# The end of a down projection on one Trainium2 core: plain products joined to the last group's PSUM sums, and a norm for each token tile

## The chip, the cores and the metric

One NeuronCore of a Trainium2 chip. The metric is the device time of one execution in microseconds (us); three runs of the kernel before took 749.31, 750.06 and 750.24 us, median 750.06 us. TensorE, VectorE, ScalarE and GpSimd appear in the profile as PE, DVE, ACT and POOL, and SP issues DMAs.

## The reference, cut to what matters

One decoder layer over 512 tokens of width 1024. The change is in the last two lines of the layer and in the final norm:

```python
u = rms_norm(h, norm_ffn_g[l])
g, up = jnp.split(u @ w_gate_up[l], 2, axis=-1)     # 1024 -> 2 x 2816
h = h + (jax.nn.silu(g) * up) @ w_down[l]           # 2816 -> 1024
return rms_norm(h, norm_final_g)                    # over the 1024 columns of each token
```

All of it is float32.

## The kernel before

Every float32 operand of a matmul is split in a high and a low part of a reduced type (fp32r), and a product is three matmuls: high by high, high by low, low by high. ScalarE writes the high part (a copy) and VectorE the low part (a subtraction). What precedes the down projection (the mixers, the output projection, 22 gate/up items) is not touched, but for one line of `gu_last`.

The hidden width of 2816 is 22 k-tiles of 128. The first 20 stand in five groups of four, `ds` 0 to 4. A group is multiplied by a seven-product scheme (Strassen's, in Winograd's form) over a 2 x 2 split: tokens in two halves (256 each), k-tiles in two, output columns in two halves of 512. Its seven products have the names of their weights, W11, S1, S2, W12, S3, S4 and W22. Of these S1 to S4 are sums of weight blocks, made by VectorE in `ds_prep` (L770), then split by ScalarE and VectorE (L775). Each product is done for two token tiles of 128 (t = 0, 1, with t + 2 in the other half) by `ds_prod`: two k-tiles by three matmuls with 512 columns. X (two PSUM tiles, `mm`) takes W11, then S2, S3 and W22 on top, and is read after each; Z (two tiles, `s`) takes S1, then S4 on top; W12 has a tile of its own (`acc`).

Groups 0 to 3 add their results to the residual in DRAM. `ds_end` is the last group, the two last k-tiles (20 and 21, `LK` = 2) and the final norm. `end_load` has brought the residual back to eight SBUF tiles `hs[t][j]` of 128 tokens by 512 columns (t = 0 to 3, j = 0, 1), and the norm's gain to `g3[j]`. In `ds_end`:

- `add_` (L975, VectorE) adds a PSUM tile, times the token's factor `r` or `nr` = -r, to an `hs` tile.
- The two last k-tiles (`LAST`, L1019 to L1030) are plain products: for each of the eight (t, j) a PSUM tile of its own, six matmuls (L1026 to L1028) and one `add_`. They stand between S2 and W12.
- The final norm goes by pairs of token tiles, (0, 1) and (2, 3). ScalarE squares each `hs` tile with a running sum. For four of the eight tiles `early` lets GpSimd multiply by the gain (L985). `rstd_pair` makes the reciprocal root of a pair (ScalarE's Ln and Exp, then Newton's step in three small VectorE instructions, L319 to L321). `apply` scales one half by root and gain on VectorE (L1000), the other, already multiplied by the gain, by the root on ScalarE, and issues the stores, 256 KB each, from SP and one of them from ScalarE.

The order is made by a scheduler at build time: `plan` lays the products out on a clock of priorities, and `at(key, product, offset)` sets the priority of what follows; each engine then works its list in that order, and waits at the first instruction that isn't ready.

Of the kernel before, what the change touches and what calls it, by code (L numbers as in the profile page):

```python
# [15 lines left out]
P = 128  # L16
# [55 lines left out]
NG = 5  # L72
DS_AFTER = {4: 0, 8: 1, 12: 2, 16: 3, 21: 4}

H_OFF, L_OFF, S_OFF, U_OFF, E_OFF, O_OFF, D_OFF = 1800, 800, 3800, 0, 3000, 1500, 1500
# [9 lines left out]
def hybrid_layer_kernel(ctx: ExitStack, tc, xT, wall, wgu, wds, wdl, g3v, vecs, wgates, consts, rope, out):  # L85
# [616 lines left out]
    def plan():  # L702

        t = 0
        seq = [(ITEMS[0], "W11")]
        for j, x in enumerate(ITEMS):
            if j == len(ITEMS) - 1:
                seq += [(x, w) for w in ("S1", "S2", "LAST", "W12", "S3", "W22", "S4")]
                continue
# [3 lines left out]
        for x, w in seq:  # L713
            clock["at"][x, w] = t
            t += 1440 if x[0] == "gu" else 8 * 680 * LK if w == "LAST" else 2720
# [42 lines left out]
    def ds_prep(n):  # L758
# [3 lines left out]
        for k in DS_W if n < NG - 1 else DS_W[:3] + (0, 1) + DS_W[3:5] + DS_W[:4:-1]:  # L762
# [3 lines left out]
            if k[0] == "S":  # L766
                a, b = {"S1": ("W21", "W22"), "S2": ("S1", "W11"), "S3": ("W11", "W21"), "S4": ("S2", "W12")}[k]
                at(key, k, -S_OFF)
# [73 lines left out]
    def gu_last(i):  # L842
# [14 lines left out]
        if i >= 4 * NG:  # L857
            V.tensor_tensor(u, u, t, op=ALU.mult)
# [103 lines left out]
    def ds_end():  # L962

        n = NG - 1
# [5 lines left out]
        v_ = lambda: small([P, 2], "v2")  # L970
        ss = {(x, j): v_() for x in (0, 2) for j in two}

        def add_(t, j, ps, c):

            V.scalar_tensor_tensor(hs[t][j], ps, c, hs[t][j], op0=ALU.mult, op1=ALU.add)  # L975

        def square(t, j):
            x = t % 2
            act_(slot(name="sq"), hs[t][j], AF.Square, accum_out=ss[t - x, j][:, x : x + 1])

        def early(t, j):

            at(key, "S4")
            square(t, j)
            nc.gpsimd.tensor_tensor(hs[t][j], hs[t][j], g3[j], op=ALU.mult)  # L985

        def rstd_pair(t0):

            v, q, z = v_(), v_(), ss[t0, 0]
            V.tensor_tensor(z, z, ss[t0, 1], op=ALU.add)  # L990
            act_(q, z, AF.Ln, scale=1.0 / D, bias=epsc)
            V.tensor_scalar(v, z, 1.0 / D, EPS, op0=ALU.mult, op1=ALU.add)
            act_(q, q, AF.Exp, scale=-0.5)
            return newton(q, v, v_)

        def apply(t0, j, q):

            for x in two:
                t, c = t0 + x, q[:, x : x + 1]
                V.scalar_tensor_tensor(hs[t][j], hs[t][j], c, g3[j], op0=ALU.mult, op1=ALU.mult)  # L1000
                act_(hs[t][1 - j], hs[t][1 - j], AF.Copy, scale=c)
                for e in two:
                    (nc.scalar if t == 3 and e != j else nc.sync).dma_start(out[t][:, e * S : e * S + S], hs[t][e])
# [15 lines left out]
        for t in range(4):  # L1019
            for j in range(2):  # L1020
                at(key, "LAST", (2 * t + j) * 1360)
                ps = mmb() if j else accb()
                q, c = slice(t * P, (t + 1) * P), slice(j * S, (j + 1) * S)
                for k in range(LK):
                    (ah, al), (wh, wl) = hid[k], DL[k]
                    T.matmul(ps, ah[:, q], wh[:, c], start=k == 0, stop=False)  # L1026
                    T.matmul(ps, ah[:, q], wl[:, c], start=False, stop=False)
                    T.matmul(ps, al[:, q], wh[:, c], start=False, stop=k == LK - 1)  # L1028
                at(key, "LAST", (2 * t + j) * 1360 + D_OFF)
                add_(t, j, ps, r[t])  # L1030
# [559 lines left out]
```

## Time and profile before

| | |
|---|---|
| three runs, median | 750.06 us (749.31 to 750.24) |
| the profiled execution, its own time | 749.53 us |
| its span, from first to last instruction | 747.8 us |
| PE busy | 734.0 us, 98% of the span, 4230 instructions |
| DVE busy | 624.0 us, 83% |
| ACT busy | 430.6 us, 58% |
| POOL busy | 66.0 us, 9% |
| mean granted clock of TensorE | 0.996 |

The span lies 1.73 us below the profiled execution's own time. The views used below are: the page's busy times; the timeline of one engine, where a row is a start, a duration, and an instruction, and a bracket gives the idle time before it and what ended it; the windows, which sum busy time over a stretch; and the groups by line. Matmuls overlap in the array: a matmul of 512 columns lasts 0.39 us from start to end, but the next one starts 0.23 us after it, so the distance between starts is what counts. The same holds on DVE and ACT, where the next start comes some 0.08 us before the end that is shown.

### The profile page before, as it was taken

How to read it: one execution, taken by the hardware profiler on the slowest of the kernel's cores; microseconds unless marked ns; L12 is line 12 of the kernel's file. 1: busy time of each engine (PE TensorE's matmuls, PEld its weight loads, DVE VectorE, ACT ScalarE, POOL GpSimd, SP SyncE). 2: the span in 40 equal slices, each digit the busy share in tenths (PEclk: the TensorE clock that was granted, in tenths of full speed). 3: DMA queues.
4: the chain of work that ended last, by engine and by line, in shares of the span. 5: the costliest groups of instructions: out<-in, count | busy, mean ns of one | idle time of the engine just before them, and what ended most of it. 6: DMA issues, size and time to landing. Idle time of an engine off the chain costs nothing.

```text
span 747.8 us, 11429 instructions
## 1 busy us (share of the span) xinstructions
PE 734.0 (98%) x4230; PEld 635.9 (85%) x4230; DVE 624.0 (83%) x1065; ACT 430.6 (58%) x739; POOL 66.0 (9%) x82
## 2 busy tenths in 40 slices
PE   9999999999999999999999999999999999999994
PEld 5788888888888888888888998899899899899983
DVE  6897776799986787566778899899999999988896
ACT  7534767578755437523447565665655765665534
POOL 0002010000000000000000000400400210220003
PEclk9999999999999999999999999999999999999998
DMA  9777654222432213524777253983985796496403
GB/s 332 270 227 206 185 178 121 101 106 78 134 135 84 85 57 104 178 96 130 188 183 194 99 163 105 231 255 74 234 251 125 180 283 157 119 251 197 140 1 113
DMA packets 50839, 118.70 MB, mean 159 GB/s; under 512 B 4944, under 2 KB 9688, under 8 KB 50784
## 3 DMA queue, kind: packets, MB, share of 16 engines
q1 hardware_dynamic: 36832, 88.82, 35.0%
q0 software_dynamic: 9440, 26.77, 18.2%
q10 hardware_dynamic: 4512, 2.39, 1.1%
q8 instruction: 33, 0.54, 0.3%
q14 instruction: 22, 0.18, 0.1%
HBM read 101.16 MB, written 16.81 MB: 158 GB/s over the span
## 4 chain that ended last, share of the span: by engine, by line
PE 94%; DVE 2%; ACT 1%; DMA 1%; issue 1%; SPq 0%; DVEq 0%; ACTq 0%
PE mm L201 12%; PE mm L202 12%; PE mm L203 12%; PE mm L783 6%; PE mm L785 6%; PE mm L784 6%; PE s L783 3%; PE s L785 3%; PE s L784 3%; PE mm L894 3%; PE mm L896 2%; PE mm L895 2%; PE mm L471 2%; PE mm L470 2%; PE acc L1309 1%; PE mm L472 1%
## 5 line engine op out<-in xcount | busy, mean ns | idle before, releaser
L148 ACT ACTIVATE wh<-raw 128x1024 fp32r<-128x1024 f32 x58 | 61.3, 1058 | 67.6 <-PE mm L202 65.0
L161 DVE TENSOR_TENSOR wl<-raw,wh 128x1024 fp32r<-128x1024 f32 x58 | 70.4, 1219 | 9.9 <-ACT wh L148 9.2
L783 PE MATMUL mm<-bq,w 128*128 128x256 f32 x264 | 76.1, 288 | 0.4
L785 PE MATMUL mm<-bq,w 128*128 128x256 f32 x264 | 74.7, 283 | 0.0
L784 PE MATMUL mm<-bq,w 128*128 128x256 f32 x264 | 74.6, 283 | 0.0
L148 ACT ACTIVATE w<-s 128x1024 fp32r<-128x1024 f32 x44 | 46.6, 1060 | 35.0 <-DVE s L740 16.2
L731 DVE TENSOR_TENSOR w<-s,w 128x1024 fp32r<-128x1024 f32 x44 | 53.8, 1222 | 9.4 <-ACT w L148 7.6
L201 PE MATMUL mm<-u,wh 128*128 128x512 f32 x136 | 55.0, 405 | 0.3 <-DVE ga L563 0.3
L693 POOL DMA_DIRECT2D s<-in_wgu_dram x22 | 19.5, 888 | 396.4 <-DVE ga L585 133.2
L203 PE MATMUL mm<-u,wh 128*128 128x512 f32 x136 | 53.3, 392 | 0.0
L783 PEld LDWEIGHTS mm<-bq,w 128*128 128x128 f32 x264 | 50.5, 191 | 3.2 <-ACT x L148 1.9
L202 PE MATMUL mm<-u,wl 128*128 128x512 f32 x136 | 53.2, 391 | 0.0
L203 PE MATMUL mm<-ul,wh 128*128 128x512 f32 x136 | 53.0, 390 | 0.0
L202 PE MATMUL mm<-uh,wl 128*128 128x512 f32 x136 | 53.0, 390 | 0.0
L201 PE MATMUL mm<-uh,wh 128*128 128x512 f32 x136 | 52.9, 389 | 0.0
L784 PEld LDWEIGHTS mm<-bq,w 128*128 128x128 f32 x264 | 50.6, 192 | 0.1
L785 PEld LDWEIGHTS mm<-bq,w 128*128 128x128 f32 x264 | 50.6, 192 | 0.0
L148 ACT ACTIVATE w<-raw 128x1024 fp32r<-128x1024 f32 (+2 forms) x45 | 43.4, 974 | 12.1 <-PE s L784 5.9
L783 PE MATMUL s<-bq,w 128*128 128x256 f32 x176 | 50.2, 285 | 0.0
L785 PE MATMUL s<-bq,w 128*128 128x256 f32 x176 | 49.9, 283 | 0.0
L784 PE MATMUL s<-bq,w 128*128 128x256 f32 x176 | 49.8, 283 | 0.0
L148 ACT ACTIVATE w<-sw 128x1024 fp32r<-128x1024 f32 x20 | 21.2, 1062 | 33.8 <-DVE sw L770 33.5
(398 smaller groups left out, 2242.1 us busy)
## 6 DMA issues: line engine op xcount, KB each, us to landing
raw<-in_wall_dram SPq DMA_DIRECT2D x59, 512.0 KB, 3.9
s<-in_wgu_dram SPq DMA_DIRECT2D x22, 512.0 KB, 4.4
s<-in_wgu_dram POOLq DMA_DIRECT2D x22, 512.0 KB, 6.1
raw<-in_wgu_dram SPq DMA_DIRECT2D x22, 512.0 KB, 4.1
raw<-in_wds_dram SPq DMA_DIRECT2D x20, 512.0 KB, 9.5
w<-in_wgu_dram SPq DMA_DIRECT2D x22, 256.0 KB, 7.6
h1d<-s POOLq DMA_DIRECT2D x16, 256.0 KB, 10.0
R<-scr POOLq DMA_DIRECT2D x4, 896.0 KB, 4.8
```

Source lines behind the costliest of these rows:

```text
L148: return A.activation(out_, in_, func, **kw)
L161: V.tensor_tensor(l, src, f(h), op=ALU.subtract)
L201: T.matmul(ps, wh[:, c], rh[j], start=start and j == 0, stop=False)
L202: T.matmul(ps, wl[:, c], rh[j], start=False, stop=False)
L203: T.matmul(ps, wh[:, c], rl[j], start=False, stop=stop and j == n - 1)
L470: T.matmul(ps, uh[k][:, c], h, start=k == 0, stop=False)
L693: nc.gpsimd.dma_start(s13, wgu[i][:, 512:1536].rearrange("p (x c) -> p x c", x=2), accum_op=ALU.add)
L731: V.tensor_tensor(dst[1], src, f(dst[0]), op=ALU.subtract)
L783: T.matmul(ps, wh[:, c], bh, start=first and k == 0, stop=False, skip_group_check=not first)
L784: T.matmul(ps, wl[:, c], bh, start=False, stop=False, skip_group_check=not first)
L785: T.matmul(ps, wh[:, c], bl, start=False, stop=k == 3, skip_group_check=not first)
L894: T.matmul(ps, bh, wh[:, d], start=first and k == 0, stop=False, skip_group_check=not first)
```

## The change

- **Plain products join sums.** In `gu_last` the hidden values of k-tiles 20 and 21 are negated for the upper 256 tokens. `last(ps, t, j)` puts the six matmuls of LAST for one (t, j) on top of a sum that is added to the same `hs` tile with the same sign anyway: (0,0) and (1,0) with W12, (0,1) and (1,1) with W22, (2,0) and (3,0) with S4. Only (2,1) and (3,1) keep a tile of their own. That of (3,1) is cut in two halves of 256 columns; the second is the last product of the kernel.
- **The end is ordered by token tile.** `ds_prod` of W22 and S4 goes tile by tile, 0, 1, 2, 3, each followed by LAST, `add_`, `square`, `rstd` and `apply` of that tile; the last product is for token tile 3.
- **A norm for each token tile.** `rstd` works on one column (128 x 1) and not two. The last square's sum goes in as the input of Ln, the other sums and epsilon as its bias.
- **Nothing on GpSimd.** `times_g` (L1007 in the new file) multiplies by the gain on VectorE.
- **Priorities.** `plan` puts W12 before S3 before LAST, with new lengths; the weight sum of the last S4 comes 10000 ahead of its product and not 3800.

The lines that are taken out stand in the functions above; these are the ones that are put in, with a line of "..." where others are left out:

```diff
-H_OFF, L_OFF, S_OFF, U_OFF, E_OFF, O_OFF, D_OFF = 1800, 800, 3800, 0, 3000, 1500, 1500
+H_OFF, L_OFF, S_OFF, U_OFF, E_OFF, O_OFF, D_OFF, S4_OFF = 1800, 800, 3800, 0, 3000, 1500, 1500, 10000
...
+        LONG = {"W12": 4, "LAST": 1, "W22": 4, "S4": 5}
-                seq += [(x, w) for w in ("S1", "S2", "LAST", "W12", "S3", "W22", "S4")]
+                seq += [(x, w) for w in ("S1", "S2", "W12", "S3", "LAST", "W22", "S4")]
-            t += 1440 if x[0] == "gu" else 8 * 680 * LK if w == "LAST" else 2720
+            t += 1440 if x[0] == "gu" else 1360 * LONG.get(w, 2) if x == ITEMS[-1] else 2720
...
-                at(key, k, -S_OFF)
+                at(key, k, -S_OFF if k != "S4" or n < NG - 1 else -S4_OFF)
...
-            V.tensor_tensor(u, u, t, op=ALU.mult)
+            V.tensor_tensor(u[:, A_], u[:, A_], t[:, A_], op=ALU.mult)
+            V.scalar_tensor_tensor(u[:, B_], u[:, B_], -1.0, t[:, B_], op0=ALU.mult, op1=ALU.mult)
...
-        at(ITEMS[-1], "LAST", -H_OFF)
+        at(ITEMS[-1], "W12", -H_OFF)
...
+        ss = {}
+        U = 1360
+        v_ = lambda: small([P, 1], "v1")
+        def add_(t, j, ps, c, d=slice(0, S)):
+            h = hs[t][j][:, d]
+            V.scalar_tensor_tensor(h, ps[:, d], c, h, op0=ALU.mult, op1=ALU.add)
+        def square(t, j, d=slice(0, S)):
+            s = v_()
+            act_(slot(name="sq")[:, d], hs[t][j][:, d], AF.Square, scale=D**-0.5, accum_out=s)
+            ss.setdefault(t, []).append(s)
+        def rstd(t, w_, o):
+            at(key, w_, o - 600)
+            *s, e = ss[t]
+            z, v, q = v_(), v_(), v_()
+            i = V.tensor_scalar(z, s[0], s[-1] if len(s) > 1 else 0.0, EPS, op0=ALU.add, op1=ALU.add)
+            at(key, w_, o)
+            act_(q, e, AF.Ln, bias=z)
+            V.tensor_tensor(v, e, z, op=ALU.add)
+            return q, v, (i, act_(q, q, AF.Exp, scale=-0.5))
+        def apply(t, q, j):
+            V.scalar_tensor_tensor(hs[t][j], hs[t][j], q, g3[j], op0=ALU.mult, op1=ALU.mult)
+            act_(hs[t][1 - j], hs[t][1 - j], AF.Copy, scale=q)
+            for e in (j, 1 - j):
+                (nc.scalar if t == 3 and e != j else nc.sync).dma_start(out[t][:, e * S : e * S + S], hs[t][e])
+        def times_g(t, j):
+            V.tensor_tensor(hs[t][j], hs[t][j], g3[j], op=ALU.mult)
+        def last(ps, t, j, first=False, d=slice(0, S)):
+            q, c = slice(t * P, (t + 1) * P), slice(j * S + d.start, j * S + d.stop)
+            for k in range(LK):
+                (ah, al), (wh, wl) = hid[k], DL[k]
+                g = dict(skip_group_check=not first)
+                T.matmul(ps[:, d], ah[:, q], wh[:, c], start=first and k == 0, stop=False, **g)
+                T.matmul(ps[:, d], ah[:, q], wl[:, c], start=False, stop=False, **g)
+                T.matmul(ps[:, d], al[:, q], wh[:, c], start=False, stop=k == LK - 1, **g)
...
         for t in two:
+            at(key, "W12", 2 * U * t)
+            y = accb()
+            last(y, t, 0, first=True)
+            ds_prod(y, w["W12"], n, 2, t)
+            at(key, "W12", 2 * U * (t + 1) + D_OFF)
+            add_(t, 0, y, r[t])
+            square(t, 0)
+        for t in two:
+            at(key, "S3", U * t)
+            ds_prod(X[t], w["S3"], n, 5, t)
+            at(key, "S3", U * t + D_OFF)
+            add_(t + 2, 1, X[t], r[t + 2])
+        for t in two:
+            at(key, "W22", U * t - 1000)
             add_(t + 2, 1, Z[t], r[t + 2])
+        at(key, "LAST")
+        y = accb()
+        last(y, 2, 1, first=True)
+        at(key, "W22", 2000)
+        add_(2, 1, y, nr[2])
+        square(2, 1)
         for t in two:
+            at(key, "W22", 2 * U * t)
             ds_prod(X[t], w["W22"], n, 6, t)
+            last(X[t], t, 1)
+            at(key, "W22", 2 * U * t + 1000)
+            times_g(t, 0)
+            at(key, "W22", 2 * U * (t + 1) + 200)
             add_(t, 1, X[t], r[t])
             square(t, 1)
+            q, v, _ = rstd(t, "W22", 2 * U * (t + 1) + 2000)
+            apply(t, newton(q, v, v_), 1)
+        at(key, "S4")
+        ds_prod(Z[0], w["S4"], n, 3, 0)
+        last(Z[0], 2, 0)
+        at(key, "S4", 1000)
+        times_g(2, 1)
+        at(key, "S4", 2 * U + 200)
+        add_(2, 0, Z[0], nr[2])
+        square(2, 0)
+        q, v, _ = rstd(2, "S4", 2 * U + 2000)
+        q2 = newton(q, v, v_)
+        y = accb()
+        lo, hi = slice(0, HS), slice(HS, S)
+        at(key, "S4", 2 * U)
+        last(y, 3, 1, first=True, d=lo)
+        at(key, "S4", 3 * U)
+        add_(3, 1, y, nr[3], lo)
+        square(3, 1, lo)
+        at(key, "S4", 5 * U // 2)
+        ds_prod(Z[1], w["S4"], n, 3, 1)
+        last(Z[1], 3, 0)
+        at(key, "S4", 9 * U // 2 + 200)
+        add_(3, 0, Z[1], nr[3])
+        square(3, 0)
+        at(key, "S4", 9 * U // 2)
+        last(y, 3, 1, first=True, d=hi)
+        at(key, "S4", 5 * U + 200)
+        add_(3, 1, y, nr[3], hi)
+        square(3, 1, hi)
+        q, v, i = rstd(3, "S4", 5 * U + 800)
+        with tc.issue_after(raw_ins(i[0])), tc.issue_after(raw_ins(i[1])):
+            apply(2, q2, 0)
+            times_g(3, 0)
+        apply(3, newton(q, v, v_), 1)
```

What the scheduler makes of it, at the three places on which the prediction rests. Names: `h_7448` to `h_7455` are hs[0][0], hs[0][1], hs[1][0] and so on to hs[3][1]; `mm_..` with h_7449, h_7451, h_7453 or h_7455 is X, `s_..` is Z, `acc_..` a tile for W12 or LAST; `sw` is a sum of weight blocks and `w` a split of one; `v` are the norm's small columns, `g` the gain.

First place, VectorE between the additions of S3 and the split of S4's weights. Before:

```order
L975 SCALAR_TENSOR_TENSOR h_7453<-mm_7608,rc_4001,h_7453 128x512
L770 TENSOR_TENSOR sw_7383<-sw_7355,raw_7097 128x1024
L975 SCALAR_TENSOR_TENSOR h_7455<-mm_7609,rc_4001,h_7455 128x512
L975 SCALAR_TENSOR_TENSOR h_7449<-mm_7608,rc_4001,h_7449 128x512
L775 TENSOR_TENSOR w_7386<-sw_7383,w_7385 128x1024
L975 SCALAR_TENSOR_TENSOR h_7451<-mm_7609,rc_4001,h_7451 128x512
L975 SCALAR_TENSOR_TENSOR h_7452<-s_7610,nrc_4002,h_7452 128x512
```

Now:

```order
L771 TENSOR_TENSOR sw_7383<-sw_7355,raw_7097 128x1024
L981 SCALAR_TENSOR_TENSOR h_7453<-mm_7606,rc_4001,h_7453 128x512
L981 SCALAR_TENSOR_TENSOR h_7455<-mm_7607,rc_4001,h_7455 128x512
L981 SCALAR_TENSOR_TENSOR h_7453<-s_7608,rc_4001,h_7453 128x512
L981 SCALAR_TENSOR_TENSOR h_7455<-s_7609,rc_4001,h_7455 128x512
L1007 TENSOR_TENSOR h_7448<-h_7448,g_7446 128x512
L981 SCALAR_TENSOR_TENSOR h_7453<-acc_7700,nrc_4002,h_7453 128x512
L981 SCALAR_TENSOR_TENSOR h_7449<-mm_7606,rc_4001,h_7449 128x512
L1007 TENSOR_TENSOR h_7450<-h_7450,g_7446 128x512
L993 TENSOR_SCALAR v_7728<-v_7664 128x1
L776 TENSOR_TENSOR w_7386<-sw_7383,w_7385 128x1024
L996 TENSOR_TENSOR v_7729<-v_7725,v_7728 128x1
```

The sum for S4 (sw_7383) stood behind X's first addition of S3 and ahead of the second; it now stands ahead of both. The split of its low part (w_7386) now stands behind the addition into h_7449, which waits for W22 and LAST of token tile 0, and two multiplies by the gain (L1007), which were GpSimd's, are in the line.

Second place, the end of TensorE's list (L894 to L896 are `ds_prod`, in the new file L897 to L899; L1015 to L1017 are `last`). Before, the last rows:

```order
L896 MATMUL s_7610<-w_7385,acl_7332 128x512
L895 MATMUL s_7611<-w_7386,ach_7058 128x512
L896 MATMUL s_7611<-w_7385,acl_7059 128x512
L894 MATMUL s_7611<-w_7385,ach_7331 128x512
L895 MATMUL s_7611<-w_7386,ach_7331 128x512
L896 MATMUL s_7611<-w_7385,acl_7332 128x512
```

Now, the last rows:

```order
L1017 MATMUL s_7609<-w_7361,acl_7512 128x512
L1015 MATMUL s_7609<-w_7365,ach_7602 128x512
L1016 MATMUL s_7609<-w_7366,ach_7602 128x512
L1017 MATMUL s_7609<-w_7365,acl_7603 128x512
L1015 MATMUL acc_7804<-w_7361,ach_7511 128x256
L1016 MATMUL acc_7804<-w_7362,ach_7511 128x256
L1017 MATMUL acc_7804<-w_7361,acl_7512 128x256
L1015 MATMUL acc_7804<-w_7365,ach_7602 128x256
L1016 MATMUL acc_7804<-w_7366,ach_7602 128x256
L1017 MATMUL acc_7804<-w_7365,acl_7603 128x256
```

Before, the last product is S4 of tile 3, and LAST is long done. Now LAST for (3, 0) follows S4 in the same PSUM tile, and the last six rows are the second half of LAST for (3, 1), 256 columns each. The first half stands 54 rows ahead, between S3 and W22. TensorE has 96 rows of 512 columns in this stretch before, and 90 of 512 and 12 of 256 now.

Third place, the end of VectorE's list. Before:

```order
L975 SCALAR_TENSOR_TENSOR h_7454<-s_7611,nrc_4002,h_7454 128x512
L319 TENSOR_TENSOR v_7785<-v_7779 128x2
L320 SCALAR_TENSOR_TENSOR v_7785<-v_7785,v_7778 128x2
L321 SCALAR_TENSOR_TENSOR v_7785<-v_7785,v_7779 128x2
L1000 SCALAR_TENSOR_TENSOR h_7449<-h_7449,v_7785,g_7447 128x512
L1000 SCALAR_TENSOR_TENSOR h_7451<-h_7451,v_7785,g_7447 128x512
L990 TENSOR_TENSOR v_7606<-v_7606,v_7607 128x2
L992 TENSOR_SCALAR v_7815<-v_7606 128x2
L319 TENSOR_TENSOR v_7821<-v_7816 128x2
L320 SCALAR_TENSOR_TENSOR v_7821<-v_7821,v_7815 128x2
L321 SCALAR_TENSOR_TENSOR v_7821<-v_7821,v_7816 128x2
L1000 SCALAR_TENSOR_TENSOR h_7452<-h_7452,v_7821,g_7446 128x512
```

Now:

```order
L319 TENSOR_TENSOR v_7800<-v_7795 128x1
L981 SCALAR_TENSOR_TENSOR h_7455<-acc_7804,nrc_4002,h_7455 128x256
L320 SCALAR_TENSOR_TENSOR v_7800<-v_7800,v_7794 128x1
L321 SCALAR_TENSOR_TENSOR v_7800<-v_7800,v_7795 128x1
L993 TENSOR_SCALAR v_7841<-v_7812,v_7828 128x1
L1001 SCALAR_TENSOR_TENSOR h_7452<-h_7452,v_7800,g_7446 128x512
L996 TENSOR_TENSOR v_7842<-v_7838,v_7841 128x1
L1007 TENSOR_TENSOR h_7454<-h_7454,g_7446 128x512
L319 TENSOR_TENSOR v_7853<-v_7843 128x1
L320 SCALAR_TENSOR_TENSOR v_7853<-v_7853,v_7842 128x1
L321 SCALAR_TENSOR_TENSOR v_7853<-v_7853,v_7843 128x1
L1001 SCALAR_TENSOR_TENSOR h_7455<-h_7455,v_7853,g_7447 128x512
```

Before, behind the last addition (h_7454) stand two Newton steps of three rows and four multiplies by root and gain, of which the last, for h_7454, follows these rows. Now the last addition is the half of h_7455, and behind it stand the rest of tile 2's Newton step and all of tile 3's, one multiply by root and gain for each of the two tiles, and one multiply by the gain alone. On the GpSimd list the four rows of L985 are gone, and nothing is put there.

## Rows read from the trace of the kernel before

**Rows 1.** The page, its first line.

```profile
span 747.8 us, 11429 instructions
```

**Rows 2.** TensorE's timeline, last 23.5 us: start, duration, instruction, idle before it.

```profile
714.49 0.39 PE L1026 MATMUL acc<-w,ach 128*128 128x512 f32 x1
...
731.97 0.39 PE L896 MATMUL mm<-w,ac 128*128 128x512 f32 x1
733.31 0.50 PE L894 MATMUL mm<-w,ac 128*128 128x512 f32 x1 [0.96 <-DVE h L975]
...
737.54 0.40 PE L896 MATMUL s<-w,acl 128*128 128x512 f32 x1
```

**Rows 3.** The timeline of TensorE's weight loads: a wait in product S4.

```profile
735.34 0.19 PEld L895 LDWEIGHTS s<-w,ach 128*128 128x128 f32 x1 [0.34 <-DVE w L775]
```

**Rows 4.** VectorE's timeline where the sum for S4 is made.

```profile
730.34 2.26 DVE L770 TENSOR_TENSOR sw<-sw,raw 128x1024 f32<-128x1024 f32 x1
732.52 1.39 DVE L975 SCALAR_TENSOR_TENSOR h<-mm,rc,h 128x512 f32<-128x512 f32 x2
```

**Rows 5.** Groups by line and form, 714 to 738: the same sum without GpSimd.

```profile
L770 DVE TENSOR_TENSOR sw<-raw,raw 128x1024 f32<-128x1024 f32 x1 | 1.2, 1217 | 0.0
```

**Rows 6.** GpSimd's timeline, three of its four multiplies by the gain.

```profile
728.91 4.82 POOL L985 TENSOR_TENSOR h<-h,g 128x512 f32<-128x512 f32 x3 [56.26 <-ACT sq L148]
```

**Rows 7.** VectorE's timeline behind the last product.

```profile
741.31 0.16 DVE L319 TENSOR_TENSOR v<-v 128x2 f32<-128x2 f32 x1 [0.40 <-ACT v L153]
...
741.90 1.42 DVE L1000 SCALAR_TENSOR_TENSOR h<-h,v,g 128x512 f32<-128x512 f32 x2
```

**Rows 8.** SP's store issues; windows (length, busy times, clock, DMA share, GB/s); landing of stores.

```profile
740.00 4.02 SPq L1003 DMA_DIRECT2D out_dram<-h  x7
740.50:741.00 0.50, 0.00 (x0) 0.00 (x0) 0.38 (x3) 0.47 (x2) 0.00 (x0) 1.00 0.29 106
742.00:743.00 1.00, 0.00 (x0) 0.00 (x0) 1.00 (x2) 1.00 (x2) 0.00 (x0) 0.62 1.04 385
746.25:746.50 0.25, 0.00 (x0) 0.00 (x0) 0.00 (x0) 0.00 (x0) 0.00 (x0) 0.50 0.42 148
DMA to landing us min/median/max: 2.0/2.5/3.2
```

**Rows 9.** VectorE's timeline: its starts where instructions follow without a wait.

```profile
713.29 0.68 DVE L858 TENSOR_TENSOR up<-up,gt 128x512 f32<-128x512 f32 x1
...
715.36 0.68 DVE L861 TENSOR_TENSOR acl<-up,ach 128x512 fp32r<-128x512 f32 x1
715.96 1.22 DVE L775 TENSOR_TENSOR w<-raw,w 128x1024 fp32r<-128x1024 f32 x1
717.10 0.74 DVE L975 SCALAR_TENSOR_TENSOR h<-acc,rc,h 128x512 f32<-128x512 f32 x1
717.76 0.74 DVE L975 SCALAR_TENSOR_TENSOR h<-mm,rc,h 128x512 f32<-128x512 f32 x1
```

**Rows 10.** TensorE's timeline, two products of 256 columns in a row.

```profile
690.28 0.28 PE L784 MATMUL acc<-bq,w 128*128 128x256 f32 x1
690.40 0.28 PE L785 MATMUL acc<-bq,w 128*128 128x256 f32 x1
```

**Rows 11.** ScalarE's timeline: the copy of a high part, a square with its sum, Ln, Exp.

```profile
720.75 1.06 ACT L148 ACTIVATE w<-sw 128x1024 fp32r<-128x1024 f32 x1 [4.81 <-DVE sw L770]
...
738.11 0.61 ACT L148 ACTIVATE sq<-h 128x512 f32<-128x512 f32 x1
738.63 0.18 ACT L148 ACTIVATION_READ_ACCUMULATOR sq<-h 128x1 f32 x1
...
740.74 0.30 ACT L153 ACTIVATE v<-v,epsc 128x2 f32<-128x2 f32 x1
741.07 0.20 ACT L153 ACTIVATE v<-v 128x2 f32<-128x2 f32 x1
```

**Rows 12.** A window over VectorE alone: length, its busy time, clock, DMA share, GB/s.

```profile
713.29:743.31 30.02, 27.26 (x43) 0.98 0.09 32
```

More of the change, by code (lines that the diff above doesn't have):

```diff
@@ L969, in ds_end @@
         g3, hs = st["h"]
[L970 to L1003, printed above, removed]
+        ss = {}
@@ L1005, in ds_end @@
         X, Z = [mmb() for t in two], [sb() for t in two]
         for t in two:
-            at(key, "W11", 1360 * t)
+            at(key, "W11", U * t)
             ds_prod(X[t], w["W11"], n, 0, t, first=True)
-            at(key, "S2", 1360 * t)
+            at(key, "S2", U * t)
             add_(t, 0, X[t], nr[t])
         for t in two:
-            at(key, "S1", 1360 * t)
+            at(key, "S1", U * t)
             ds_prod(Z[t], w["S1"], n, 1, t, first=True)
         for t in two:
-            at(key, "S2", 1360 * t)
+            at(key, "S2", U * t)
@@ L1016, in ds_end @@
             ds_prod(X[t], w["S2"], n, 4, t)
-            at(key, "S2", 1360 * t + 2720)
+            at(key, "W12", U * t)
             add_(t + 2, 0, X[t], nr[t + 2])
[L1019 to L1030, printed above, removed]
@@ L1031, in ds_end @@
-        for t in two:
-            at(key, "W12")
-            add_(t + 2, 1, Z[t], r[t + 2])
-        for t in two:
-            at(key, "W12", 1360 * t)
-            y = accb()
-            ds_prod(y, w["W12"], n, 2, t, first=True)
-            at(key, "S3", 1360 * t)
-            add_(t, 0, y, r[t])
-            early(t, 0)
-        for t in two:
-            at(key, "S3", 1360 * t)
-            ds_prod(X[t], w["S3"], n, 5, t)
-            add_(t + 2, 1, X[t], r[t + 2])
-            early(t + 2, 1)
@@ L1046, in ds_end @@
-        for t in two:
-            at(key, "W22", 1360 * t)
+        for t in two:
+            at(key, "W12", 2 * U * t)
[10 more added lines that the diff above has]
+            add_(t + 2, 1, X[t], r[t + 2])
@@ L1049, in ds_end @@
             add_(t, 1, X[t], r[t])
             square(t, 1)
-        at(key, "S4", -1000)
-        q = rstd_pair(0)
-        for t in two:
-            at(key, "S4", 1360 * t)
-            ds_prod(Z[t], w["S4"], n, 3, t)
-            add_(t + 2, 0, Z[t], nr[t + 2])
-            square(t + 2, 0)
-        at(key, "S4", 1360 * 3)
-        apply(0, 1, q)
-        at(key, "S4", 3000)
-        apply(2, 0, rstd_pair(2))
+            q, v, _ = rstd(t, "W22", 2 * U * (t + 1) + 2000)
+            apply(t, newton(q, v, v_), 1)
```

## The prediction, as put on record before the run

> **What bounds the kernel now.** I read the end of the trace backwards, in four views. The reader is to see one stretch after another in which a different thing is late. The span ends at 747.8 us [rows 1]. Stores: the eight output stores of 256 KB are issued from 740.00 on, and the DMA engines run full, at 385 GB/s, until the last bytes: the window from 746.25 still moves 148 GB/s, that is, 0.10 us at full rate, so the last byte goes at 746.35 [rows 8]. 1.45 us later the span ends. Norm: TensorE's last product ends at 737.94 [rows 2]; two Newton steps and four multiplies follow, and the last multiply ends at 743.32 [rows 7]. That is 5.38 us behind TensorE, and 4.48 us before the end. Products: ahead of that TensorE works almost without a gap. From 714.49 to 731.97 there are 77 distances between starts, 0.227 us each [rows 2]; 96 products at that distance, and 0.16 us for the last to drain, would take 21.95 us, and took 23.45. So 1.50 us are lost, in two places: 0.96 us before the product at 733.31, released by an addition on VectorE [rows 2], and 0.34 us at the weight load at 735.34, released by the split of S4's weights on VectorE [rows 3]; the rest is the slow start after them.
>
> Both losses have one cause. The sum of weight blocks at 730.34 took 2.26 us [rows 4], and the same instruction took 1.22 us where GpSimd was idle [rows 5]. In those microseconds GpSimd multiplied by the gain [rows 6]. Without the extra 1.04 us the addition behind it, into X, would have ended about when TensorE came to need it, 732.2.
>
> **The change, part by part.**
>
> *Products.* The columns stay the same: 90 products of 512 at 0.227 us and 12 of 256 at 0.12 us [rows 10] make 21.87 us, 0.08 us more than 96 of 512. If TensorE waits for nothing, it ends at 714.49 + 21.87 + 0.16 = 736.52. Bounds: 736.5, and 738.0 if all that is lost now is lost again. I walked VectorE's new line to choose, with the distances of its kinds [rows 9]: 0.60 us for 512 elements, 1.14 for 1024, 0.66 for an addition or a multiply by root and gain; small ones 0.2, three in 0.59 [rows 7]. The anchor is 713.29, where the old line starts u for the last k-tile [rows 9]; up to there the new one is the same.
>
> - W22 needs X free. 42 rows of 512 and six of 256 stand ahead of W22, so TensorE wants it at 724.74. On VectorE stand ahead: the product u (0.67), a split (1.14), the low part of the hidden (0.60), two additions (1.32), a sum (1.14), an addition (0.66): 718.82. The next split waits until ScalarE has copied the high part, 1.06 us [rows 11] from the sum's end at 718.2 on: 719.3. Then 1.14, 0.66, 1.14, 1.14 and 0.66 lead to 724.1. Slack 0.6 us.
> - S4's low weights now stand behind the addition into h_7449, which waits for TensorE itself. From the end of that sum TensorE has 14 more rows before it needs them, 3.0 us after draining; VectorE needs 0.03 + 0.66 + 0.60 + 0.2 + 1.22 = 2.7 us. Slack 0.3 us.
>
> Both are thin but positive, so I take 736.5.
>
> *VectorE's load.* Seven additions go, and one more becomes two halves (0.7 against 0.66): -4.6 us. The multiplies of GpSimd come, 4 x 0.60 = +2.4. Twenty small instructions stand where ten did: +2.0. The longer sum goes: -1.0. The split of u in two: +0.07. Together about -1.1 us. That looks free, but it is not slack: the line now runs from 713.29 with six of 1024 (6.84), seventeen of 0.66 (11.2), five of 0.60 (3.0), halves (1.4) and twenty small (4.0), 26.4 us, and would be done at 739.7 if it never waited. In the old one VectorE is busy 27.26 of 30.02 us [rows 12].
>
> A rule speaks against this part. The old rows show GpSimd carrying 1.61 us for each multiply, three in 4.82 [rows 6], beside a VectorE that is nearly always busy [rows 12]. The Trainium skill, page "Perfetto Trace Analysis", section "Optimizing Scalar/DVE Operations", says that a saturated DVE is helped by giving work to ScalarE or even GpSimd and by grouping small operations, though it adds that GpSimd and DVE share a read port. By that rule the move and the doubled small instructions would cost what they add to a full line; by the rows they are paid for by the seven additions. The rule returns as a rival below.
>
> *Norm.* Counted from TensorE's end. VectorE comes to the last half addition at +0.15, since the addition of (3, 0) and a small one are ahead, and ends it at +0.57 (0.42: half of an addition is not in these rows; bounds 0.33 and 0.75). ScalarE is busy with the square of (3, 0), 0.61 + 0.18 [rows 11], to +0.74. A square of 256 has no row either; between half of one of 512 with its sum, 0.40, and the whole, 0.79, I take 0.50, nearer to the half: +1.24. Ln 0.30 and Exp 0.20 [rows 11], with 0.03 each: +1.80. VectorE meanwhile works off tile 2: from +0.49 on three small, a multiply (0.66), one small, the multiply by the gain (0.60), so it is free at +2.55, later than Exp. Newton 0.59 and the last multiply 0.75: +3.9. Bounds: 3.0 if nothing of tile 2 is in the way, 5.4 as now. I take 3.9, so the last data stand at 740.4.
>
> *Stores.* Six of eight stores are issued while TensorE or the norm still works; they cost the path nothing, unless they run into the last two. From first issue to first byte it takes 0.86 us (740.00, and a window with 106 GB/s, 0.14 us at full rate, before 741.00) [rows 8]. Two stores of 256 KB at 385 GB/s take 1.36, and the end follows 1.45 later: 3.67 us instead of 4.48. Bounds: 3.1 (the fastest landing of one store, 2.0 us, and 1.1 for issue and end, an estimate from the old end, whose last issue stops at 744.02 and whose longest landing is 3.2 us [rows 8]) and 4.5.
>
> *Elsewhere.* The two extra VectorE instructions in `gu_last` (0.07 each) lie in a stretch where VectorE has idle time behind them or a split ahead of TensorE's need; nothing. No DMA is added, and none moves ahead of another's need.
>
> **The sum.** 736.5 + 3.9 + 3.7 = 744.1 us of span against 747.8, a gain of 3.7: 1.4 from the products, 1.5 from the norm, 0.8 from the stores. The profiled execution took 749.53 itself, so it would take 745.8; the median of the runs shown is 0.53 above it. I go half way, as for each time below, and say **746.1**. Differences below 0.2%, 1.5 us, can't be told from no change.
>
> **Rivals.**
>
> 1. *VectorE becomes the bound.* This is the Trainium skill's rule from above made a mechanism. The old line waited 2.8 us in its 30.02 [rows 12]; my sum lets the new one wait about 0.7 (740.4 less 739.7). If it waits as much as the old, the last data stand 2 us later, at 742.4, and the gain shrinks to 1.7: 748.1. For it: slacks of 0.3 and 0.6 us; against it: the old waits were for products that now come in another order. Chance 0.13.
> 2. *The stores gain nothing,* since the last two are queued behind others: 746.9. For it: the queue was full in the old end; against it: 1.4 us of transfers are left then, and 2 us pass between tile 2's stores and the last. Chance 0.08.
> 3. *Slower: the four roots stop VectorE.* Each root is addition, square, Ln, Exp, then Newton: 0.03 + 0.75 + 0.03 + 0.79 + 0.03 + 0.30 + 0.03 + 0.20 = 2.2 us, of which VectorE itself works 0.66. If the Newton step of a tile stands right behind its addition, VectorE stops for 1.5 us, and all that is behind it too, S4's additions and the next roots. Four times that, 6 us, less the 0.40 that shows now [rows 7], takes the 3.7 away and 1.9 more: 751.7. It decides from the point where less than 1.5 us of other VectorE work stands between. In the order 2.8 us stand behind tile 0's addition, 3.3 behind tile 1's, 2.3 behind tile 2's and 2.1 behind tile 3's. Chance 0.04.
> 4. *No change:* TensorE's losses come back elsewhere, 738.0, and the norm takes 5 us: 746.7 of span, 748.7. Chance 0.05.
>
> **How the numbers follow.** The forecast has 0.70. Its own range is 744.9 (the norm at its lower bound, 0.9 less, and 0.3 off the stores) to 747.0 (0.9 more of thin slacks). To leave out at most 2 in 10 the range reaches over rivals 1 and 2: **744.9 to 748.3**. Faster by over 0.2%, below 748.56: all of the forecast, rival 2, and four fifths of rival 1: 0.88. Same: the rest of rival 1 and rival 4: 0.08. Slower 0.04.
>
> **What would show it.** Right: no idle time of TensorE over 0.3 us behind 714; the weight sum at 1.2 us; no GpSimd row at the end; last product within 0.3 us of 736.5; last multiply within 0.5 of 740.4; six stores issued before it. Wrong: a TensorE wait on an addition or on the split of S4's weights; VectorE rows of the norm with idle time behind Ln or Exp; the DMA engines full when the last two stores are issued.

## The result, and the profile after

The changed kernel takes **745.88 us** (median of 6 runs, 745.64 to 746.34) where the kernel before takes 749.71 (6 runs, 749.31 to 750.24): a ratio of **0.9949**, 95% interval 0.9936 to 0.9962. The predicted time was 746.1. The profiled execution took 745.64 itself; the head of its page, with the busy time of each engine:

```profile
span 743.9 us, 11459 instructions
PE 733.4 (99%) x4236; PEld 636.7 (86%) x4236; DVE 622.2 (84%) x1076; ACT 431.7 (58%) x745; POOL 59.3 (8%) x78
```

It is 3.9 us shorter than before [rows 1]. I cut the end of every run into the three stretches of the prediction: **products** (from the start of the first plain product into `acc` to the end of TensorE's last product), **norm** (on to the end of VectorE's last multiply), **stores** (on to the end of the span). A span is given to 0.1 us, so the last stretch is good to 0.05 us.

TensorE's timeline after the change, start and duration: the first plain product, the first of W22, the product that first reads S4's low weights, the last one:

```profile
714.39 0.39 PE L1015 MATMUL acc<-w,ach 128*128 128x512 f32 x1
...
724.62 0.40 PE L897 MATMUL mm<-w,ac 128*128 128x512 f32 x1
...
730.54 0.39 PE L898 MATMUL s<-w,ach 128*128 128x512 f32 x1
...
736.12 0.28 PE L1017 MATMUL acc<-w,acl 128*128 128x256 f32 x1
```

The timeline of the weight loads, at that S4 product:

```profile
730.32 0.19 PEld L898 LDWEIGHTS s<-w,ach 128*128 128x128 f32 x1
```

No row of either timeline has idle time before it from 714.39 on: both waits of before [rows 2, 3] are gone. 736.40 less 714.39 is 22.01 us, 1.44 less than before. VectorE's timeline where TensorE used to be stopped:

```profile
722.26 1.22 DVE L771 TENSOR_TENSOR sw<-sw,raw 128x1024 f32<-128x1024 f32 x1
723.39 1.41 DVE L981 SCALAR_TENSOR_TENSOR h<-mm,rc,h 128x512 f32<-128x512 f32 x2
...
728.90 1.22 DVE L776 TENSOR_TENSOR w<-sw,w 128x1024 fp32r<-128x1024 f32 x1
```

The sum takes 1.22 us where it took 2.26 [rows 4]. The first of the two additions out of X ends at about 724.1, 0.5 us before W22; S4's low weights stand at 730.12, 0.2 us before the weight load. VectorE's timeline around and behind the last product:

```profile
735.73 0.75 DVE L981 SCALAR_TENSOR_TENSOR h<-s,nrc,h 128x512 f32<-128x512 f32 x1 [0.43 <-PE s L1017]
736.40 0.15 DVE L319 TENSOR_TENSOR v<-v 128x1 f32<-128x1 f32 x1
736.46 0.47 DVE L981 SCALAR_TENSOR_TENSOR h<-acc,nrc,h 128x256 f32<-128x256 f32 x1
736.86 0.15 DVE L320 SCALAR_TENSOR_TENSOR v<-v,v 128x1 f32<-128x1 f32 x1
...
737.40 0.74 DVE L1001 SCALAR_TENSOR_TENSOR h<-h,v,g 128x512 f32<-128x512 f32 x1
738.06 0.15 DVE L996 TENSOR_TENSOR v<-v,v 128x1 f32<-128x1 f32 x1
738.13 0.69 DVE L1007 TENSOR_TENSOR h<-h,g 128x512 f32<-128x512 f32 x1
738.73 0.15 DVE L319 TENSOR_TENSOR v<-v 128x1 f32<-128x1 f32 x1
738.91 0.16 DVE L320 SCALAR_TENSOR_TENSOR v<-v,v 128x1 f32<-128x1 f32 x1
...
739.30 0.75 DVE L1001 SCALAR_TENSOR_TENSOR h<-h,v,g 128x512 f32<-128x512 f32 x1
```

ScalarE's timeline there: the last square, Ln, Exp.

```profile
737.14 0.40 ACT L148 ACTIVATE sq<-h 128x256 f32<-128x256 f32 x1
737.45 0.19 ACT L148 ACTIVATION_READ_ACCUMULATOR sq<-h 128x1 f32 x1
737.66 0.29 ACT L153 ACTIVATE v<-v,v 128x1 f32<-128x1 f32 x1
737.99 0.20 ACT L153 ACTIVATE v<-v 128x1 f32<-128x1 f32 x1
```

The window over VectorE alone that answers to [rows 12]:

```profile
713.29:740.05 26.76, 25.08 (x52) 0.98 0.15 55
```

Exp of tile 3 is done at 738.19, but VectorE comes to its Newton step only at 738.73, behind tile 2's multiply and the multiply by the gain. The last multiply ends at 740.05, 3.65 us behind TensorE (5.38 before). SP's issues of stores:

```profile
733.02 7.39 SPq L1004 DMA_DIRECT2D out_dram<-h  x7
```

Windows, columns as in [rows 8]:

```profile
740.50:741.00 0.50, 0.00 (x0) 0.00 (x0) 0.00 (x0) 0.00 (x0) 0.00 (x0) 0.50 0.15 53
...
742.25:742.50 0.25, 0.00 (x0) 0.00 (x0) 0.00 (x0) 0.00 (x0) 0.00 (x0) 0.50 0.24 74
```

Six stores go out from 733.0 on, the last two at 740.05 (ScalarE) and 740.08 (SP), and from 740.5 to 741.0 the DMA engines stand almost idle: nothing queues ahead of the last two. Their last byte goes at 742.30 (74 GB/s for 0.25 us is 0.05 us at 385), the end comes 1.60 us later.

### The profile page after: what moved, and what is told of

Read it like the earlier page. It is cut to its first block, busy times and chain, and to the rows that moved or that the text cites. A ratio compares the mean times of both kernels' runs of the same rounds, so it can differ in the third digit from the quotient of the medians.

```text
span 743.9 us, 11459 instructions
## 1 busy us (share of the span) xinstructions
PE 733.4 (99%) x4236; PEld 636.7 (86%) x4236; DVE 622.2 (84%) x1076; ACT 431.7 (58%) x745; POOL 59.3 (8%) x78
## 4 chain that ended last, share of the span: by engine, by line
PE 95%; DVE 2%; ACT 1%; DMA 1%; issue 1%; SPq 0%; DVEq 0%; ACTq 0%
PE mm L201 12%; PE mm L202 12%; PE mm L203 12%; PE mm L784 6%; PE mm L786 6%; PE mm L785 6%; PE s L784 3%; PE s L786 3%; PE s L785 3%; PE mm L897 3%; PE mm L898 2%; PE mm L899 2%; PE mm L470 1%; PE mm L471 1%; PE acc L785 1%; PE acc L784 1%
```

## The experiments

All columns but the last two in us, from each profiled execution. The first plain product started anywhere from 714.39 to 715.59, in the changed kernel itself at 714.39 and, run again (after_again), at 715.04. That lateness is much older than anything the change touches. One and the same product near the start, in the changed kernel and in its second run:

```profile
11.16 0.39 PE L203 MATMUL mm<-u,w 128*128 128x512 f32 x1
11.90 0.40 PE L203 MATMUL mm<-u,w 128*128 128x512 f32 x1
```

So kernels are compared by the sum of the three stretches; the ratio is against the kernel before in the same series.

| kernel | products | norm | stores | sum | median us | ratio, 95% |
|---|---|---|---|---|---|---|
| before | 23.45 | 5.38 | 4.48 | 33.31 | 749.71 | |
| changed | 22.01 | 3.65 | 3.85 | 29.51 | 745.88 | 0.9949 (0.9936 to 0.9962) |
| b_no_gain | 22.43 | 5.36 | 4.49 | 32.28 | 748.99 | 0.9987 (0.9978 to 0.9996) |
| b_early_sum | 21.95 | 5.68 | 4.42 | 32.05 | 748.55 | 0.9983 (0.9974 to 0.9992) |
| b_gain_on_dve | 22.78 | 5.71 | 4.36 | 32.85 | 749.49 | 0.9996 (0.9987 to 1.0005) |
| a_gain_on_pool | 23.28 | 4.08 | 3.80 | 31.16 | 748.05 | 0.9976 (0.9967 to 0.9986) |
| a_one_gain_on_pool | 22.01 | 4.04 | 3.76 | 29.81 | 747.12 | 0.9962 (0.9950 to 0.9975) |
| a_late_sum | 22.01 | 3.66 | 3.82 | 29.49 | 746.31 | 0.9950 (0.9937 to 0.9962) |
| a_unjoined | 23.89 | 4.73 | 3.79 | 32.41 | 749.51 | 0.9992 (0.9983 to 1.0001) |
| a_no_half | 21.92 | 3.62 | 3.78 | 29.32 | 746.08 | 0.9943 (0.9930 to 0.9957) |
| a_late_stores | 22.01 | 3.66 | 5.89 | 31.56 | 748.28 | 0.9979 (0.9970 to 0.9988) |
| a_pair_norm | 22.01 | 4.46 | 4.35 | 30.82 | 747.70 | 0.9967 (0.9956 to 0.9979) |
| a_newton2_first | 22.01 | 3.31 | 3.74 | 29.06 | 745.60 | 0.9943 (0.9931 to 0.9956) |
| after_again | 22.01 | 3.65 | 3.80 | 29.46 | 746.47 | 0.9953 (0.9940 to 0.9965) |

**GpSimd out of the kernel before** (b_no_gain). The multiply in `early`, line 985, is dropped.

> The kernel before, with the four multiplies by the gain on GpSimd left out (part of the output is then not scaled). Theory (the products' 1.5 us were lost because GpSimd's multiplies stretched the weight sum): the sum takes 1.2 us instead of 2.26, the gap of 0.96 us ahead of the addition into X goes, the last product ends at 736.5 to 736.9 instead of 737.94, and all behind it keeps its length; span 746.3 to 746.8 for 747.8, ratio 0.998 to 0.9987. Rival (VectorE simply has too many additions ahead of the one into X): the gap keeps more than half its length, span 747.3 or more, ratio above 0.9993.

VectorE's sum, and the timeline of the weight loads for W22 and S4:

```profile
730.75 1.22 DVE L770 TENSOR_TENSOR sw<-sw,raw 128x1024 f32<-128x1024 f32 x1
732.68 0.19 PEld L894 LDWEIGHTS mm<-w,ac 128*128 128x128 f32 x1 [0.34 <-DVE h L975]
734.74 0.19 PEld L895 LDWEIGHTS s<-w,ach 128*128 128x128 f32 x1 [0.37 <-DVE w L775]
```

The sum took 1.22 us, the products 22.43: 1.02 of the 1.50 us lost are regained. The other half microsecond is not: two waits for VectorE remain, 0.34 us for the addition out of X behind the sum and 0.37 us for the split of S4's weights, about as long as before (0.34). Norm and stores kept their length. In the stretches 1.03 us are gained, in the ratio 0.0013: the theory's side, at its small end (the span, 747.2, lies above its 746.8, with a start 0.43 us later).

**Only the sum earlier** (b_early_sum).

```diff
-                at(key, k, -S_OFF)
+                at(key, k, -S_OFF if k != "S4" or n < NG - 1 else -10000)
```

> The kernel before, with S4's weight sum alone made as early as in the changed kernel, ahead of GpSimd's multiplies. Theory: the sum takes 1.2 us, TensorE's two waits go although VectorE keeps all its additions, the last product ends at 736.4 to 736.9; but norm and stores stay as they are, 5.4 and 4.5 us behind it, so the span is 746.3 to 746.8, ratio 0.998 to 0.9987: less than half of the change's gain of 3.9. Rival (additions, not contention): VectorE is as full as before, TensorE waits at another addition, gain under 0.5 us. Second rival (contention only moves): another VectorE instruction with both inputs in SBUF, the split of S4's weights, is stretched by GpSimd by 0.5 us or more.

VectorE's timeline of this kernel:

```profile
727.13 1.22 DVE L770 TENSOR_TENSOR sw<-sw,raw 128x1024 f32<-128x1024 f32 x1
...
732.22 1.21 DVE L775 TENSOR_TENSOR w<-sw,w 128x1024 fp32r<-128x1024 f32 x1
...
736.24 0.87 DVE L990 TENSOR_TENSOR v<-v,v 128x2 f32<-128x2 f32 x1
```

GpSimd's timeline, its last three multiplies:

```profile
732.48 4.61 POOL L985 TENSOR_TENSOR h<-h,g 128x512 f32<-128x512 f32 x3 [0.68 <-ACT sq L148]
```

One offset in the kernel before saves all 1.5 us of the products, with every addition still on VectorE, so the additions as such did not cost them. The offset does two things at once: the sum no longer runs beside GpSimd, and it no longer stands between the two additions out of X. With b_no_gain the two can be parted: the stretch was worth 1.0 us, the place the remaining 0.5. The split of S4's weights, begun 0.26 us ahead of GpSimd, was not stretched. But the second rival is right in part, the contention moved: an instruction of two columns took 0.87 us where it takes 0.15 in the kernel before, and ended at 737.11 when GpSimd ended at 737.09; norm lost 0.30. (The span, 747.0, is 0.2 above the theory's, with a start 0.46 us later.)

**Only the multiplies moved** (b_gain_on_dve). `nc.gpsimd.tensor_tensor` becomes `V.tensor_tensor` in `early`.

> The kernel before, with the four multiplies by the gain on VectorE instead of GpSimd, nothing else. Theory: the sum shrinks by 1.04 us, but four multiplies of 0.60 stand in VectorE's line, 2.4 us more; the waits of TensorE shrink by less than the whole, and what VectorE is late behind TensorE's end grows; together -0.6 to +1.0 us, ratio 0.999 to 1.0015: the move of the multiplies does not pay by itself, only with the additions that were taken away. Rival (taking GpSimd out is the whole of it): the span falls by 1.0 us or more, ratio below 0.9988.

As the theory has it: the sum fell to 1.22 us, but W22's weight load still waited 0.34 us for the addition, the load of S4's weights now 0.70 us for its split, and the norm took 0.33 more. 0.46 us gained, no difference in the ratio.

**The multiplies given back to GpSimd, all or one** (a_gain_on_pool, a_one_gain_on_pool).

```diff
-            V.tensor_tensor(hs[t][j], hs[t][j], g3[j], op=ALU.mult)
+            nc.gpsimd.tensor_tensor(hs[t][j], hs[t][j], g3[j], op=ALU.mult)
```
```diff
-            times_g(3, 0)
+            nc.gpsimd.tensor_tensor(hs[3][0], hs[3][0], g3[0], op=ALU.mult)
```

> The changed kernel, with its four multiplies by the gain on GpSimd again. Theory: VectorE sheds 2.4 us, but the last of them, for tile 3, can only start when the square has read its data, about 737.3, and takes 1.6 us, and an instruction of VectorE with both inputs in SBUF that runs beside one is stretched by up to a microsecond; TensorE may wait again where S4's low weights have only 0.4 us of slack. Span 743.5 to 745.0 for 743.9; ratio to the kernel before 0.9945 to 0.9965. Rival (a full VectorE is what ends the kernel, so the gain belongs on the idle GpSimd): the last multiply ends 0.5 us earlier or more, span 743.3 or less, ratio below 0.9943.

> The changed kernel, with the last multiply by the gain alone, that of tile 3, on GpSimd. In the changed kernel tile 3's Newton step waited behind it: Exp ended at 738.19, Newton began at 738.73. Theory (VectorE's line sets the end): Newton begins at 738.2 to 738.3, the last multiply ends at 739.5 to 739.6 instead of 740.05, GpSimd is done at about 738.9, before ScalarE needs it; span 743.4 to 743.5. Rival (contention eats it): VectorE's multiply by root and gain for tile 2, both inputs in SBUF, runs beside GpSimd and is stretched by 0.5 us or more; span 743.8 or more.

All four: 1.65 us worse than the changed kernel, more than either side expected. GpSimd's timeline:

```profile
720.74 1.72 POOL L1007 TENSOR_TENSOR h<-h,g 128x512 f32<-128x512 f32 x1 [47.41 <-ACT sq L148]
722.80 1.89 POOL L1007 TENSOR_TENSOR h<-h,g 128x512 f32<-128x512 f32 x1 [0.34 <-ACT sq L148]
```

VectorE's timeline beside it:

```profile
721.88 1.66 DVE L776 TENSOR_TENSOR w<-raw,w 128x1024 fp32r<-128x1024 f32 x1
723.46 2.31 DVE L771 TENSOR_TENSOR sw<-sw,raw 128x1024 f32<-128x1024 f32 x1
```

TensorE's timeline, its one wait:

```profile
726.58 0.47 PE L897 MATMUL mm<-w,ac 128*128 128x512 f32 x1 [1.04 <-DVE h L981]
```

They read as taking turns. The split at 721.88 starts while GpSimd works, and ends 1.08 us after GpSimd's 722.46, close to its usual 1.22. GpSimd's next starts at 722.80 in the middle of the split and ends at 724.69, 1.15 us after it; the sum started at 723.46 and ends 1.08 after that. TensorE then waits 1.04 us for the addition behind the sum, as before the change.

The one for tile 3 alone, GpSimd's timeline:

```profile
738.22 1.26 POOL L1097 TENSOR_TENSOR h<-h,g 128x512 f32<-128x512 f32 x1 [66.37 <-ACT sq L148]
```

VectorE's timeline beside it:

```profile
738.30 1.73 DVE L1001 SCALAR_TENSOR_TENSOR h<-h,v,g 128x512 f32<-128x512 f32 x1
```

Here the rival was right: tile 2's multiply by root and gain, 0.75 us elsewhere, took 1.73, and the norm is 0.39 longer instead of 0.5 shorter. Its own time is 1.64 us above the changed kernel's: 0.30 of that is in the stretches, 0.90 is a later start, of which 0.70 stand already at the product of 11.16 us, and 0.44 lies outside the span; why is not shown.

**The sum's place in the changed kernel** (a_late_sum: `S4_OFF` 3800 for 10000).

> The changed kernel, with S4's weight sum due where it was before instead of 6.2 us earlier. Theory: with no GpSimd work at the end the sum takes 1.2 us wherever it stands, so its place is worth little: TensorE's waits stay under 0.5 us together, span 743.7 to 744.6 for 743.9. Rival (the early place is what took TensorE's waits away): waits of 0.8 us or more come back at the addition into X or at S4's weights, span 744.7 or more.

Nothing changes, 29.49 us for 29.51: with GpSimd out and the products joined, the place is worth nothing. In the kernel before, with GpSimd out and all additions in (b_no_gain), it was still worth 0.5.

**Sums not joined** (a_unjoined). Six products get an `acc` tile and an addition of their own; one of the four places:

```diff
-        last(Z[0], 2, 0)
+        y = accb()
+        last(y, 2, 0, first=True)
...
         add_(2, 0, Z[0], nr[2])
+        add_(2, 0, y, nr[2])
```

> The changed kernel, but the products of the last two k-tiles do not join the group's sums: six of them keep PSUM tiles of their own and six more additions of 0.66 us go to VectorE, 4.0 us on a line that waits only some 2 us from 713.29 on. Theory: VectorE becomes the bound; TensorE waits for it or the last multiply comes 2 to 4 us later than 740.05; span 746 to 748, so at least half of the gain is lost. Rival (tile order and the lone norms give the gain, the joined sums hardly anything): span below 745.

TensorE's timeline shows the wait:

```profile
720.05 0.50 PE L1015 MATMUL acc<-w,ach 128*128 128x512 f32 x1 [1.58 <-DVE h L981]
```

2.90 of the 3.80 us are lost: 1.9 in the products, 1.1 in the norm. The wait is for an addition that frees one of the two `acc` tiles; so PSUM tiles and VectorE's six additions are both in it, and this run doesn't part them.

**No halves** (a_no_half). `last(y, 3, 1)` whole with its gain ahead of S4 of tile 3, the later half gone, `apply(3, ..., 0)`.

> The changed kernel without the cut of the last plain product into halves: (3, 1) whole ahead of S4 of tile 3, and (3, 0) the last. Worked out: the last product ends 0.08 us earlier; addition 0.75, square 0.73, Ln 0.30, Exp 0.20 and the gaps put Exp at +2.1 instead of +1.8 behind TensorE, Newton and the last multiply follow; but VectorE has no multiply by the gain left there and is free at about +2.1 as well. Theory (VectorE's line behind the last product, not Ln and Exp, sets the end): within 0.3 us of the changed kernel, span 743.6 to 744.3. Rival (the chain addition, square, Ln, Exp sets it, and the halves shorten it): 0.5 us later or more, span 744.4 or more.

Norm 3.62 for 3.65, products 21.92 for 22.01: the halves are worth nothing. Exp ends at +2.21 us behind the last product, not +1.79, but VectorE comes to the Newton step at +2.29, about as before (+2.33). The span, 744.4, touches the rival's bound only by a start 0.69 us later.

**Stores held back** (a_late_stores): `apply` keeps the stores of tiles 0 and 1, and SP issues them behind tile 2's first.

> The changed kernel, with the four stores of tiles 0 and 1 held back on SP behind the first store of tile 2, so that seven of the eight are issued from 738.2 on instead of one after another from 733.0. Theory (the early stores are out of the way of the last two, and that is worth something only because the DMA engines are full when stores come together): eight stores are then 5.4 us of transfer at 385 GB/s behind a first byte at about 739.0, last byte at 744.5, the end 1.5 us later; 2 us or more longer than the changed kernel from the last product to the end, 9.5 us or more for 7.5. Rival (the last store's own fixed time sets the end, not the queue): under 0.5 us longer.

SP's issues:

```profile
739.22 0.34 SPq L1007 DMA_DIRECT2D out_dram<-h  x1
739.61 2.01 SPq L1011 DMA_DIRECT2D out_dram<-h  x4
741.72 1.88 SPq L1007 DMA_DIRECT2D out_dram<-h  x2
```

The window with the last bytes:

```profile
745.50:746.00 0.50, 0.00 (x0) 0.00 (x0) 0.00 (x0) 0.00 (x0) 0.00 (x0) 0.50 0.16 57
```

9.55 us from the last product to the end for 7.50, the last byte at 745.57, as the theory has it: what is queued ahead of the last stores decides.

**Tiles 2 and 3 normed as a pair** (a_pair_norm): one Ln, Exp and Newton step on two columns, then both `apply`.

> The changed kernel, with tiles 2 and 3 normed together as before (one Ln, one Exp, one Newton step of two columns, then two multiplies), all else as changed. Theory (VectorE's work behind the last product is what counts): a Newton step and some small instructions fall away and the multiply by the gain moves into idle time, but the multiply of tile 2 moves behind Exp; the last multiply ends 0.2 to 0.6 us later behind the last product than the 3.65 us of the changed kernel, and four stores come together, which costs the end 0.4 to 0.8 us; from the last product to the end 8.1 to 8.9 us for 7.5. Rival (a norm for each tile alone is the bulk of the 1.7 us saved behind the last product): the last multiply at 4.7 us or more, the end at 9.2 or more.

8.81 us, in the theory's span, but 0.81 of the 1.31 lost are in the norm, more than the 0.2 to 0.6 worked out: 4.46 lies between the theory's 4.25 and the rival's 4.7. The lone norm of the last tile is worth 0.8 and its effect on the stores 0.5.

**Tile 2's Newton step in the idle time** (a_newton2_first). The core of it, besides tile 1's copy behind tile 2's Exp:

```diff
+        with tc.issue_after(raw_ins(n2[0])):
+            add_(3, 0, Z[1], nr[3])
...
+        with tc.issue_after(raw_ins(n2[1])):
+            i = add_(3, 1, y, nr[3], hi)
+        with tc.issue_after(raw_ins(i)):
+            i = apply(2, q2, 0, "V")
```

> The changed kernel, with tile 2's Ln and Exp ahead of ScalarE's copy for tile 1, two of tile 2's three Newton instructions in the 0.43 us in which VectorE waits for the addition of (3, 0), and tile 2's multiply right behind the last half addition. Theory (VectorE's line behind the last product sets the end): the last multiply ends 0.1 to 0.45 us sooner behind the last product than 3.65 us, and the end comes as much sooner; under 0.06% of the time, so the medians agree within their interval. Rival (the chain square, Ln, Exp of tile 3 sets it): no change, since the addition of (3, 0) starts later.

> The changed kernel once more, on the chip of the three runs beside it, as their base: 22.0, 3.65 and 3.85 us from the first plain product to the last product, to the last multiply, to the end, each within 0.1; the start of the first plain product may differ by up to a microsecond, since it stands at 714.4 to 715.6 in the runs so far.

The changed kernel, run again, kept its stretches: 22.01, 3.65 and 3.80 us. ScalarE's Exp and VectorE's Newton step in a_newton2_first:

```profile
738.79 0.20 ACT L153 ACTIVATE v<-v 128x1 f32<-128x1 f32 x1
739.03 0.16 DVE L319 TENSOR_TENSOR v<-v 128x1 f32<-128x1 f32 x1
```

Norm 3.31 for 3.65, sum 29.06 for 29.46 in the changed kernel beside it. Exp ends later than there, at +1.94 us behind the last product (737.05) for +1.79, and still the end comes sooner: VectorE's line did set it. Now the Newton step follows Exp by 0.04 us, so here ScalarE's chain has become as long as VectorE's line. The medians are 745.60 and 746.47, the intervals of the ratios overlap: the lowest median, by less than these runs can tell.

## Why the prediction was right, step by step

**Products**, 736.52 forecast, 736.40 measured; 1.4 us forecast, 1.44 gained. The number came from a walk along VectorE's new line, and the walk was right: the slacks of 0.6 and 0.3 us were 0.5 and 0.2 (to the weight load). The account of the old losses was too simple. "Both losses have one cause" holds for 1.0 of the 1.5 us: with GpSimd's multiplies out and all else kept, the sum is back at 1.22 us and waits of 0.34 and 0.37 us remain (b_no_gain). They go when the sum is moved (b_early_sum), or when the products are joined and GpSimd is out, at either place of the weight sum (a_late_sum). [rows 5], "the same instruction", is another sum of the same size; the trace after has the sum itself at 1.22 us.

The forecast spoke of contention; the runs say more: VectorE and GpSimd take turns. A multiply that goes first takes GpSimd 1.26 to 1.30 us. In the kernel before, GpSimd's second and third multiply, and VectorE's addition out of PSUM beside the first two:

```profile
730.22 1.29 POOL L985 TENSOR_TENSOR h<-h,g 128x512 f32<-128x512 f32 x1
731.47 2.26 POOL L985 TENSOR_TENSOR h<-h,g 128x512 f32<-128x512 f32 x1
729.67 0.75 DVE L975 SCALAR_TENSOR_TENSOR h<-mm,rc,h 128x512 f32<-128x512 f32 x1 [0.29 <-PE mm L896]
```

The sum begins at 730.34, beside the second multiply, and ends at 732.60 [rows 4], 1.09 us after that multiply's end at 731.51; the third multiply ends 1.13 us after the sum. So the "1.61 us" for each multiply [rows 6] holds GpSimd's own wait. The addition, which has one operand in PSUM, was not stretched. The Trainium skill, page "SBUF — State Buffer", section "SBUF: two separate sides", says just this: a VectorE operation with two SBUF inputs and a GpSimd operation that reads SBUF lock each other out for a whole instruction, and whichever starts first goes on. The rows above agree: 1.66, 2.31, 0.87 and 1.73 us for 1.22, 1.22, 0.15 and 0.75, each ending behind GpSimd's end.

**VectorE's load**, 26.4 us of busy time forecast, 25.08 measured. The term that was off is the twenty small instructions at 0.2 us: 4.0 forecast, about 2.7 left of the 25.08 if the others took the 22.4 forecast for them. Only one that needs the result just before it costs 0.18 to 0.20 (738.73 to 738.91). One that doesn't, behind a large one, costs 0.07 (738.06 to 738.13). The other sum of that part, -1.1 us net, counts one addition too many: of twenty additions six go and one is halved, -3.9 us and not -4.6, and about -0.45 net; the forecast does not rest on it. The first rival, VectorE as the bound with the last data at 742.4, did not come: of 26.76 us it waits 1.7, not 0.7, and the last data stand at 740.05. That the joined products pay for the moved multiplies fits a_unjoined, which loses 2.90 with six additions back (and PSUM tiles with them), and b_gain_on_dve, the move alone, which gains nothing measurable. The Trainium skill, page "Perfetto Trace Analysis", section "Optimizing Scalar/DVE Operations", says that unloading a full VectorE onto ScalarE or even GpSimd may make sense, but between VectorE and GpSimd might not help, for their shared port; here giving back one multiply cost 0.30 us and four 1.65, so the caveat decides.

**Norm**, +3.9 forecast, 3.65 measured. The chain was right to 0.03: square of 256 columns in 0.50, Exp at +1.79 for +1.80. The half addition, 0.42 forecast, ran 0.47. VectorE came free at +2.33 for +2.55, again the small instructions. That VectorE, not Exp, sets the end is shown by a_newton2_first; the halves don't shorten it (a_no_half). Of the 1.73 us gained, a_pair_norm shows where 0.81 come from; the rest is not parted by a run.

**Stores**, 3.67 forecast, 3.85 measured: first byte and transfer as forecast (742.27 against 742.30), but the end follows the last byte by 1.60 us, not 1.45. The second rival falls: the queue was empty for the last two, and a_late_stores shows what a full one costs.

**The roots' rival**, a VectorE stopped four times: its longest wait behind the roots is 0.43 us, for TensorE.

**The sum.** The gains are 1.44, 1.73 and 0.63 us for 1.4, 1.5 and 0.8 forecast. The misses of norm and stores, 0.25 less and 0.18 more, nearly cancel; that 746.1 lies so close to 745.88 is partly luck, and the same kernel run again has a median of 746.47.

## What to carry to other kernels

When an instruction takes much longer than its like, look at the other engine in those microseconds before counting load, and then at the instruction's place in its line: b_early_sum got a third of this gain from one offset. Work moved off a helper engine must be paid for on the receiving one; count its line with dependent and independent small instructions apart. Behind the last product, the queue of the engine that works off the tail, and stores sent as soon as each tile is done, count for more than cutting the last product finer.

## What was not expected of the hardware

A blocked VectorE instruction need not be large: one of two columns stood 0.7 us behind GpSimd. Small instructions behind a large one cost 0.07 us of VectorE's line, dependent ones 0.19. The start of the same stretch differed by up to 1.2 us between executions in which TensorE works the same list up to there. In the changed kernel run again, 0.74 us of lateness stand at the product of 11.16 us and 0.65 at the first plain product; between 8 and 14 us the DMA engines are full in both traces (402 GB/s). Why one execution comes out of that stretch later than the other is not shown.
